# First out-projection tile written out by hand with its own w_out stages; context-convolution taps and gate products kept in written order

## The chip, the cores and the metric

The kernel runs on one core of a Trainium2 chip. A core has five engines with queues of their own: TensorE (PE, matrix products), VectorE (DVE), ScalarE (ACT), GpSimd (POOL) and SyncE (SP, which here issues most of the transfers). Each engine works through its own list of instructions in order; between engines, semaphores hold an instruction until what it needs is there. The metric is the device time of one execution in microseconds, and lower is better. The kernel before takes 1871.06 us in the median of 3 runs (1869.57 to 1874.34).

## What is computed

One layer of a hybrid network on 256 context tokens and 2048 latent tokens, all in float32. An input projection gives six groups of columns; a state-space branch (SSD, with a short convolution and two scan directions) and a conformer branch (a gated convolution of width 31 and a layer norm) are computed from them and meet in one output projection with w_out:

```python
h = rms_norm(x, g_pre) * (1 + scale) + shift
u = h @ w_in
z, xbc, dt_raw, ga, gb, gsil = jnp.split(u, [I_Z, I_XBC, I_DT, I_GA, I_GB], axis=-1)
y_ssd, h_fin = ssd_branch(z, xbc, dt_raw, ssd_conv_w, ssd_conv_b, a_log, dt_bias, d_skip, ssd_norm_g, h0)
y_conf = conformer_branch(ga.reshape(bsz, rows, cols, D_CONF), gb.reshape(bsz, rows, cols, D_CONF),
                          conf_conv_w, conf_conv_b, conf_ln_g, conf_ln_b)
y_conf = y_conf.reshape(bsz, seqlen, D_CONF) * jax.nn.silu(gsil)
out = jnp.concatenate([y_ssd, y_conf], axis=-1) @ w_out
return x + gate * rms_norm(out, g_post), h_fin
...
def conformer_branch(ga, gb, conv_w, conv_b, ln_g, ln_b):
    h = ga * jax.nn.sigmoid(gb)
    h = depthwise_conv(h, conv_w, conv_b)
    h = layer_norm(h, ln_g, ln_b)
    return jax.nn.silu(h)
```

The outputs are the context rows, the latent rows and the final states of the context's two scans.

## The kernel before

The 2304 tokens are 18 tiles of 128 (0 and 1 are context) and, for the input projection, five blocks (`TOK`, `BNS`: one of 256 tokens, four of 512) in two halves, `ORDER = ((1, 2, 0), (3, 4))`. A float32 product is three products of rounded parts (high by high, low by high, high by low; L391 to L393 in the input projection, `out_part`, L1136, in the output projection, where all instructions of the stage carry L77, the line of the helper that records them). So each operand is cast (ACT) and its rest subtracted (DVE).

For each half the columns come in units of 128: the xbc columns with their 5-tap convolution, then `gab_unit` (eight units; gb, then ga for each block, with the product gth at L555), then `silu_unit` for z and gs (L567, L568). `load_w` brings the columns: in the first half from w_in, split on the chip and kept in DRAM; in the second half by two loads wh and wl (L359, L360) from there. Beside these units generators run in alternation: the scan of the SSD branch (L663 to L795), the latent convolution on PE (cp, L648, evicted by DVE as cvv, L652, and stored at L657), `gate_rows` (products of w_mod columns wg for the gate, L576 to L581) and `ctx_conv` (L600 to L613: for each of eight channel groups, cg is loaded at L602, the first tap is L606 and thirty more are L608, all on DVE).

The scheduler of the language decides the order of each engine's list from a simulated time line, and may move one instruction ahead of another that was written first. The exception is what is recorded through `InOrder` while its flag `on` is set: that stays behind the instruction of its engine recorded before it. The flag is set for the loop over output tiles only (L1243 on).

Behind the second half, `w_out` is brought in 16 row blocks k by `load_wo` (L965 to L977): a load to wst, a cast to woh on ACT, a subtraction to wol on DVE. Blocks 0 to 8 are loaded before the three last silu units (gs columns 5 to 7, run first over block 3 for all three, then over block 4); blocks 9 to 15 at L1224, behind them, when the buffers of the input projection are closed. The tiles of the output projection run from 17 down. Each needs, for its SSD half, the state product qo and decay, the gate with z, the squares' sums over channels (zr, then pm on PE, rstd, pn on PE), and for its conformer half cn, its mean (cm), centring, squares (nq), scale, silu and the gate with gs. Tile 17 is prepared among and behind the last silu units, tile 16 behind them (L1226 to L1242); every later tile is prepared in the loop while its predecessor's 16 k-steps run on PE. The state of the backward context scan is written at the very end (`state_out(1, ...)`, L1316).

PSUM has 3 banks for the unit products ("mm") and 5 for the rest. `SLOT = (0, 1, 2, 1, 2)` says in which of three buffers a block's input lies; such a buffer is closed when the last unit that reads it has run, and its room goes to the pools of the output projection (p2 for the conformer tiles, p3 for output tiles).

## Time and profile before

| what | value |
|---|---|
| median of 3 runs | 1871.06 us (1869.57 to 1874.34) |
| the profiled execution, its own time | 1872.28 us |
| span of the profiled execution | 1870.5 us |
| mean granted TensorE clock | 0.984 |
| ACT busy, POOL busy | 863.8 us (46%), 175.9 us (9%) |
| HBM traffic over the span | 200 GB/s |
| last stage, last silu matmul to the end | 1404.90 to 1870.5 us |

The page lists each engine's busy time. PE is a list of matmuls that follow each other at a fixed pitch; where it stands still, the waits view names the tile that it wanted and the instruction or transfer that gave it. A row of the timeline is start, duration, engine, line and operation, output<-inputs, and in brackets the idle time ahead of it with what ended it. The windows view cuts the span into stretches. Its column PEclk is the clock that TensorE was granted as a share of full speed. SPq rows are DMA issues on SP's queue.

### The profile page before, as it was taken

How to read it: one execution, taken by the hardware profiler on the slowest of the kernel's cores; microseconds unless marked ns; L12 is line 12 of the kernel's file. 1: busy time of each engine (PE TensorE's matmuls, PEld its weight loads, DVE VectorE, ACT ScalarE, POOL GpSimd, SP SyncE). 2: the span in 40 equal slices, each digit the busy share in tenths (PEclk: the TensorE clock that was granted, in tenths of full speed). 3: DMA queues.
4: the chain of work that ended last, by engine and by line, in shares of the span. 5: the costliest groups of instructions: out<-in, count | busy, mean ns of one | idle time of the engine just before them, and what ended most of it. 6: DMA issues, size and time to landing. Idle time of an engine off the chain costs nothing.

```text
span 1870.5 us, 30012 instructions
## 1 busy us (share of the span) xinstructions
PE 1808.1 (97%) x11223; PEld 1493.1 (80%) x11223; DVE 1203.1 (64%) x1841; ACT 863.8 (46%) x1956; POOL 175.9 (9%) x281
## 2 busy tenths in 40 slices
...
GB/s 298 219 199 210 203 241 181 175 254 219 195 217 211 226 196 169 167 155 189 170 200 233 199 251 229 258 244 175 331 189 209 183 167 174 172 171 178 182 106 79
DMA packets 305309, 375.22 MB, mean 201 GB/s; under 512 B 85254, under 2 KB 204678, under 8 KB 305164
## 3 DMA queue, kind: packets, MB, share of 16 engines
...
q14 instruction: 57, 0.47, 0.1%
HBM read 243.66 MB, written 129.59 MB: 200 GB/s over the span
## 4 chain that ended last, share of the span: by engine, by line
PE 85%; DMA 7%; DVE 4%; ACT 1%; issue 1%; SPq 1%; POOL 0%; POOLq 0%; DVEq 0%; ACTq 0%
PE op L77 21%; PE sp L391 7%; PE sp L392 7%; PE sp L393 7%; PE xp L391 5%; PE xp L392 5%; PE xp L393 5%; PE ga L391 3%; PE ga L393 2%; PE ga L392 2%; PE gb L391 2%; PE gb L393 2%; PE gb L392 2%; DMA lb<-lt 2%; PE py L732 2%; DVE cg L608 2%
## 5 line engine op out<-in xcount | busy, mean ns | idle before, releaser
L696 ACT ACTIVATE lb<-lb,WB 128x128 f32<-128x128 f32 x576 | 184.3, 391 | 167.7 <-POOL lb L688 162.1
L391 PE MATMUL sp<-hh,wh 128*128 128x512 f32 (+1 forms) x640 | 238.5, 373 | 0.0
L392 PE MATMUL sp<-hl,wh 128*128 128x512 f32 (+1 forms) x640 | 236.0, 369 | 0.0
L393 PE MATMUL sp<-hh,wl 128*128 128x512 f32 (+1 forms) x640 | 235.8, 368 | 0.0
L391 PE MATMUL xp<-hh,wh 128*128 128x512 f32 (+1 forms) x480 | 179.3, 375 | 6.1 <-ACT wh L366 4.9
L688 POOL TENSOR_SCALAR_AFFINE_SELECT lb<-lb 128x512 f32<-128x512 f32 x144 | 112.6, 786 | 714.2 <-ACT el L685 366.7
L393 PE MATMUL xp<-hh,wl 128*128 128x512 f32 (+1 forms) x480 | 179.0, 373 | 0.0
L392 PE MATMUL xp<-hl,wh 128*128 128x512 f32 (+1 forms) x480 | 178.9, 373 | 0.0
L488 DVE SCALAR_TENSOR_TENSOR cva<-raw,cwh,cva 128x1280 f32<-128x1280 f32 (+1 forms) x96 | 142.1, 1488 | 19.7 <-ACT cva L482 17.9
L391 PEld LDWEIGHTS sp<-hh,wh 128*128 128x128 f32 x640 | 120.6, 189 | 20.8 <-DVE sth L568 0.4
L393 PEld LDWEIGHTS sp<-hh,wl 128*128 128x128 f32 x640 | 120.6, 188 | 20.7
L392 PEld LDWEIGHTS sp<-hl,wh 128*128 128x128 f32 x640 | 120.7, 189 | 19.8
L391 PE MATMUL ga<-hh,wh 128*128 128x512 f32 (+1 forms) x320 | 122.0, 381 | 6.8 <-DMA wh<-whd 6.3
L391 PE MATMUL gb<-hh,wh 128*128 128x512 f32 (+1 forms) x320 | 121.4, 379 | 5.3 <-DVE gth L555 5.3
L393 PE MATMUL ga<-hh,wl 128*128 128x512 f32 (+1 forms) x320 | 119.4, 373 | 0.5 <-DMA wl<-wld 0.5
L392 PE MATMUL gb<-hl,wh 128*128 128x512 f32 (+1 forms) x320 | 119.6, 374 | 0.0
L393 PE MATMUL gb<-hh,wl 128*128 128x512 f32 (+1 forms) x320 | 119.6, 374 | 0.0
L392 PE MATMUL ga<-hl,wh 128*128 128x512 f32 (+1 forms) x320 | 119.2, 373 | 0.0
L568 DVE SCALAR_TENSOR_TENSOR sth<-sth,sp 128x512 f32<-128x512 f32 (+1 forms) x80 | 50.4, 630 | 97.3 <-ACT sth L567 96.9
L391 PEld LDWEIGHTS xp<-hh,wh 128*128 128x128 f32 x480 | 92.1, 192 | 23.2 <-ACT wh L366 5.5
L608 DVE SCALAR_TENSOR_TENSOR cg<-cg,cv 128x256 f32<-128x256 f32 x240 | 107.6, 487 | 0.6
L392 PEld LDWEIGHTS xp<-hl,wh 128*128 128x128 f32 x480 | 91.7, 191 | 15.7 <-DVE hl L312 0.4
...
## 6 DMA issues: line engine op xcount, KB each, us to landing
lb<-lt ACTq DMA_DIRECT2D x144, 256.0 KB, 4.5
...
```

The lines of the kernel that those rows point to most:

```text
L77: return lambda *a, **k: self._tc.keep_in_program_order(f(*a, **k))
L391: T.matmul(ps[:, :BN], wh[:, k, :], hh[:, k, :], start=(k == 0), stop=False)
L392: T.matmul(ps[:, :BN], wh[:, k, :], hl[:, k, :], start=False, stop=False)
L393: T.matmul(ps[:, :BN], wl[:, k, :], hh[:, k, :], start=False, stop=(k == KT - 1))
L488: V.scalar_tensor_tensor(a[:, :n], raw[:, t:t + n], cwh[:, ct * 5 + t:ct * 5 + t + 1], a[:, :n], MUL, ADD)
L568: V.scalar_tensor_tensor(th, th, 1.0, ps[:, :BN], ADD, MUL)
L608: V.scalar_tensor_tensor(acc, g[:, t:t + 256], cv[:, w0 + t:w0 + t + 1], acc, MUL, ADD)
L688: G.affine_select(E[g, hq, d], E[g, hq, d], pattern=[[0, 4], [sg, P]], compare_op=ALU.is_ge, fill=NEG, base=0, channel_multiplier=-sg)
L696: S.activation(lb[:, h, :], lb[:, h, :], AF.Exp, bias=WB[:, i, c + h:c + h + 1])
L732: T.matmul(py[g][j * HD:(j + 1) * HD, q * P:(q + 1) * P], xt[g][:, h * HD:(h + 1) * HD], E[g, hq, 0][:, t, :], start=True, stop=True)
```

## The change

1. `InOrder` gets `here`, which keeps one instruction in written order without the flag. The gate products and the taps of `ctx_conv` use it.
2. `SLOT` becomes (0, 1, 2, 2, 1): blocks 3 and 4 exchange their buffers. The last two z units of the first half run over blocks 2, 1, 0 in place of 1, 2, 0, and the last silu units of the second half over block 4 first and then block 3, so that block 4, with tiles 14 to 17, is finished one pass earlier, and p2 is opened between the two passes.
3. `load_wo` is cut into `wo_load` and `wo_split`, and w_out 9 to 15 get staging buffers of p3.
4. Tile 16's SSD part and both conformer tiles' loads, sums, means and squares are written among the last silu units, tile 15's SSD loads too.
5. The first output tile is written out ahead of the loop, with the splits of w_out 9 to 15 between its k-steps. In the second and third tile (`e` 4 and 2) the stages come 4 and 2 k-steps later than in the rest.
6. `state_out(1, ...)` is written inside the tile before the last.

```diff
-SLOT = (0, 1, 2, 1, 2)
+SLOT = (0, 1, 2, 2, 1)
...
+    def here(self, name, *a, **k):
+        return self._tc.keep_in_program_order(getattr(self._eng, name)(*a, **k))
...
-                    V.scalar_tensor_tensor(acc[a][:, :D], wg, sc[:, a, k:k + 1], acc[a][:, :D], MUL, ADD)
+                    V.here("scalar_tensor_tensor", acc[a][:, :D], wg, sc[:, a, k:k + 1], acc[a][:, :D], MUL, ADD)
...
-            V.scalar_tensor_tensor(acc, g[:, t:t + 256], cv[:, w0 + t:w0 + t + 1], acc, MUL, ADD)
+            V.here("scalar_tensor_tensor", acc, g[:, t:t + 256], cv[:, w0 + t:w0 + t + 1], acc, MUL, ADD)
...
+            tag = ("gg", "xr", "o", "o")[k % 4]
+            wst[k] = p3.tile([P, D], F32, tag=tag, name=f"wst{k}", bufs=2 if tag == "o" else 1)
...
+    i1 = order[1]
+    ssd_load(i1)
+    st_load(i1)
...
-    last = [silu_unit(1, GS0, GS, j, hb) for j in range(5, 8)]
+    last = [silu_unit(1, GS0, GS, j, hb, (4, 3)) for j in range(5, 8)]
     for b in range(2):
         for m, u in enumerate(last):
             run(take(u, 8))
             if b == 0 and m == 1:
                 rs = norms(i, yz, None)
-            if b == 1 and m == 0:
+                state_mm(i1)
+                y_state(i1)
+                y_gate(i1)
+            if b == 0 and m == 2:
                 ssd_scale(i, yz[0], spread(i, rs))
                 yh = hl(p0, "y", 2, i, yz[0])
                 lo(yh)
+                yz = y_sum(i1)
...
                 ph_b[1].close()
                 p2 = ph_1.enter_context(tc.tile_pool(name="p2", bufs=1))
-                n = conf_load(i)
-                v, t = conf_sum(i, n)
-                conf_centre(n, conf_mean(i, t))
+                nn = [conf_load(i), conf_load(i1)]
+                vv = [conf_sum(j, n) for j, n in zip((i, i1), nn)]
...
+                nq = conf_sqsum(i, vv[0][0])
+            if b == 1 and m == 0:
+                rs = norms(i, None, nq)
+                nq = conf_sqsum(i1, vv[1][0])
...
-    for k in range(9, 16):
-        load_wo(k, wo4)
+    for k in range(9, 13):
+        wo_load(k, wo4)
...
+    banks(i)
+    out_part(pso[i], yh, 0, 1)
+    rs = norms(nxt, yz, nq)
+    out_part(pso[i], yh, 1, 4)
...
+    out_part(pso[i], yh, 5, 8)
+    for k in (9, 10):
+        wo_split(k)
+        wo_load(k + 4, wo4)
+    v = nq[0]
+    conf_silu(n, v)
+    out_part(pso[i], pt, 8, 9)
+    v2, t = conf_sum(nx2, n2)
+    wo_split(11)
+    wo_load(15, wo4)
+    for k in range(12, 15):
+        wo_split(k)
+    load_gg(0)
+    out_part(pso[i], pt, 9, 12)
+    mean = conf_mean(nx2, t)
+    y_state(nx2)
+    state_decay(nx2, 0)
+    wo_split(15)
...
+    for a, i in enumerate(order[1:], 1):
         last = a + 1 == NT
+        e = {1: 4, 2: 2}.get(a, 0)
...
+        out_seg(i, yh, pt, 8 + e, 10 + e)
+        if a + 2 == NT:
+            state_out(1, Sb, lambda n: p1.tile([P, D], F32, tag="z", name=n, bufs=2)[:, 0:512])
...
-    state_out(1, Sb, lambda n: p1.tile([P, D], F32, tag="z", name=n, bufs=2)[:, 0:512])
```

Each engine has the same number of instructions as before. Three places of the lists follow; a row is line, operation, output<-inputs and shape, and lines from L75 on stand some lines further down in the changed kernel (L77 there is L81, L555 is L559; `here` is L75).

PE's list before, from the end of the last silu unit on (pm and pn are the sums and the spread of the norms of tile 17 or 16, qo16 tile 16's state product, cm16 its mean, op17 the first output tile, zr16 and nq16 the sums of tile 16's squares):

```order
L1059 MATMUL pm17_13676<-ones_218,nq17_13672 128x1
L1070 MATMUL pn17_13682<-ident_209,yr171_13680 128x128
L1014 MATMUL qo160_13762<-ct16_13749,Sb0_13062 128x128 x4
L1014 MATMUL qo161_13763<-ct16_13749,Sb1_13063 128x128 x4
L1107 MATMUL cm16_13801<-v16_13797,ones_218 128x128
L77 MATMUL op17_0_13822<-woh0_13065,yh17_13584 128x512
L77 MATMUL op17_1_13823<-woh0_13065,yh17_13584 128x512
L77 MATMUL op17_0_13822<-wol0_13064,yh17_13584 128x512
L77 MATMUL op17_1_13823<-wol0_13064,yh17_13584 128x512
L77 MATMUL op17_0_13822<-woh0_13065,yl17_13585 128x512
L77 MATMUL op17_1_13823<-woh0_13065,yl17_13585 128x512
L77 MATMUL pm16_13833<-ones_218,zr16_13777 128x1
```

PE's list in the changed kernel: first the piece between two of the silu units over block 4, where tile 16's state product now stands; then the end of the last silu unit.

```order
L397 MATMUL sp1_4640_6_4_13507<-hh4_7330,wl5408_1_13416 128x512
L1072 MATMUL pm17_13532<-ones_218,zr17_13284 128x1
L1027 MATMUL qo160_13538<-ct16_13306,Sb0_13062 128x128 x4
L1027 MATMUL qo161_13539<-ct16_13306,Sb1_13063 128x128 x4
L395 MATMUL sp1_4640_7_4_13553<-hh4_7330,wh5536_1_13479 128x512
```

```order
L397 MATMUL sp1_4640_7_3_13725<-hh3_7120,wl5536_1_13478 128x512
L81 MATMUL op17_0_13791<-woh0_13065,yh17_13581 128x512
L1072 MATMUL pm17_13662<-ones_218,nq17_13629 128x1
L1083 MATMUL pn17_13701<-ident_209,yr171_13666 128x128
L81 MATMUL op17_1_13792<-woh0_13065,yh17_13581 128x512
L81 MATMUL op17_0_13791<-wol0_13064,yh17_13581 128x512
L81 MATMUL op17_1_13792<-wol0_13064,yh17_13581 128x512
L81 MATMUL op17_0_13791<-woh0_13065,yl17_13582 128x512
L81 MATMUL op17_1_13792<-woh0_13065,yl17_13582 128x512
L81 MATMUL pm16_13799<-ones_218,zr16_13585 128x1
L81 MATMUL pm16_13799<-ones_218,nq16_13668 128x1
L81 MATMUL op17_0_13791<-woh1_13091,yh17_13581 128x512
```

The norm of tile 17's conformer half now stands within the first k-step, and the state product and mean of tile 16 no longer stand ahead of it; the sums pm16 still stand behind the first k-step.

DVE's list before, in the first half, around the first tap (L606) of the third channel group, cg2, and the product gth of the gab unit 3, block 2:

```order
L773 TENSOR_TENSOR yg11_2948<-yg11_2948,py11_3150 128x512
L606 TENSOR_SCALAR cg2_4773<-cg2_4773,cv_214,cfb2_250 128x256
L775 TENSOR_TENSOR yg11_2948<-yg11_2948,yo11_3225 128x512
L608 SCALAR_TENSOR_TENSOR cg2_4773<-cg2_4773,cv_214 128x256 x2
L795 TENSOR_TENSOR btl2_3299<-pb2_3228,bth2_3298 128x256
L608 SCALAR_TENSOR_TENSOR cg2_4773<-cg2_4773,cv_214 128x256
L721 TENSOR_TENSOR xw200_3424<-xt20_3304,WS_259 128x512
L555 SCALAR_TENSOR_TENSOR gth0_3_2_3195<-gth0_3_2_3195,ga0_3_2_3197 128x512
L608 SCALAR_TENSOR_TENSOR cg2_4773<-cg2_4773,cv_214 128x256
```

The same place in the changed kernel:

```order
L777 TENSOR_TENSOR yg11_2948<-yg11_2948,py11_3150 128x512
L779 TENSOR_TENSOR yg11_2948<-yg11_2948,yo11_3225 128x512
L799 TENSOR_TENSOR btl2_3299<-pb2_3228,bth2_3298 128x256
L725 TENSOR_TENSOR xw200_3424<-xt20_3304,WS_259 128x512
L559 SCALAR_TENSOR_TENSOR gth0_3_2_3195<-gth0_3_2_3195,ga0_3_2_3197 128x512
L705 TENSOR_TENSOR lb2000_3170<-lb2000_3170,cb2_3300 128x512
L705 TENSOR_TENSOR lb2010_3246<-lb2010_3246,cb2_3300 128x512
L705 TENSOR_TENSOR lb2100_3327<-lb2100_3327,cb2_3300 128x512
L727 TENSOR_TENSOR xwl200_3426<-xw200_3424,xwh200_3425 128x512
L772 TENSOR_TENSOR yg21_3519<-xT2_3102,dcol_246 128x512
```

The first tap of the third group and its followers are no longer here; in the changed list they stand behind the last taps of group two.

DVE's list before, early in the second half's gab units, between two product rows gth; cvv0 is the eviction of the latent convolution's product cp0:

```order
L608 SCALAR_TENSOR_TENSOR cg4_8920<-cg4_8920,cv_214 128x256
L608 SCALAR_TENSOR_TENSOR cg5_10011<-cg5_10011,cv_214 128x256
L652 SCALAR_TENSOR_TENSOR cvv0_8673<-cp0_0_8674,cbb_8324 128x8x64
L652 SCALAR_TENSOR_TENSOR cvv0_8673<-cp0_1_8675,cbb_8324 128x8x64
L608 SCALAR_TENSOR_TENSOR cg4_8920<-cg4_8920,cv_214 128x256
L608 SCALAR_TENSOR_TENSOR cg5_10011<-cg5_10011,cv_214 128x256
```

And in the changed kernel, from the same state product's operand xwl901 on:

```order
L727 TENSOR_TENSOR xwl901_8640<-xw901_8638,xwh901_8639 128x512
L725 TENSOR_TENSOR xw910_8768<-xt91_8584,WS_259 128x512
L559 SCALAR_TENSOR_TENSOR gth1_1_3_8510<-gth1_1_3_8510,ga1_1_3_8512 128x512
L656 SCALAR_TENSOR_TENSOR cvv0_8673<-cp0_0_8674,cbb_8324 128x8x64
L656 SCALAR_TENSOR_TENSOR cvv0_8673<-cp0_1_8675,cbb_8324 128x8x64
L755 TENSOR_TENSOR Sf0_260<-Sf0_260,eTf_253 128x512
L757 TENSOR_TENSOR yo90_8882<-po90_8759,el90_8426 128x512
L759 TENSOR_TENSOR Sf0_260<-Sf0_260,pst900_8764 128x512
L727 TENSOR_TENSOR xwl910_8770<-xw910_8768,xwh910_8769 128x512
L725 TENSOR_TENSOR xw911_8885<-xt91_8584,WS_259 128x512
L704 TENSOR_TENSOR lb10000_8950<-lb10000_8950,lb10001_8952 128x512
L656 SCALAR_TENSOR_TENSOR cvv0_8673<-cp0_2_8790,cbb_8324 128x8x64
```

There are sixteen alternating taps of the groups cg4 and cg5 in front of cvv0 before, of which the fence shows the last two; in the changed kernel cvv0 stands straight behind gth1_1_3.

More of the change, by code (lines that the diff above doesn't have):

```diff
@@ L919, in backbone_kernel @@
     interleave(post(0, 6), merge(scan(range(9)), 68, extra, 9 + 4 * 13), 90 * 8)
-    last = [silu_unit(0, GS0, GS, j, hb, (1, 2, 0)) for j in (6, 7)]
+    last = [silu_unit(0, GS0, GS, j, hb, (2, 1, 0)) for j in (6, 7)]
     prep = hprep(3, hb)
@@ L963, in backbone_kernel, with wo_load, wo_split @@
     WH, WL = {}, {}
-    def load_wo(k, pool):
-        wl = pool.tile([P, D], F32R, name=f"wol{k}", tag=f"wol{k}")
-        wh = pool.tile([P, D], F32R, name=f"woh{k}", tag=f"woh{k}")
-        wr = p0.tile([P, D], F32, tag=("yh", "yl")[k % 2], name=f"wst{k}", bufs=2)
-        DMA.dma_start(wr, w_out[k * P:(k + 1) * P, :])
+    wst = {}
+    def wo_load(k, pool):
+        WL[k] = pool.tile([P, D], F32R, name=f"wol{k}", tag=f"wol{k}")
+        WH[k] = pool.tile([P, D], F32R, name=f"woh{k}", tag=f"woh{k}")
+        if k < 9:
+            wst[k] = p0.tile([P, D], F32, tag=("yh", "yl")[k % 2], name=f"wst{k}", bufs=2)
+        else:
+            tag = ("gg", "xr", "o", "o")[k % 4]
+            wst[k] = p3.tile([P, D], F32, tag=tag, name=f"wst{k}", bufs=2 if tag == "o" else 1)
+        DMA.dma_start(wst[k], w_out[k * P:(k + 1) * P, :])
+    def wo_split(k):
+        wl, wh, wr = WL[k], WH[k], wst.pop(k)
         if k < 8:
@@ L1207, in backbone_kernel @@
                 lo(yh)
+                yz = y_sum(i1)
+                for g in range(2):
+                    state_decay(i1, g)
                 ph_b[1].close()
                 p2 = ph_1.enter_context(tc.tile_pool(name="p2", bufs=1))
-                n = conf_load(i)
-                v, t = conf_sum(i, n)
-                conf_centre(n, conf_mean(i, t))
+                nn = [conf_load(i), conf_load(i1)]
+                vv = [conf_sum(j, n) for j, n in zip((i, i1), nn)]
+                for (v, t), j, n in zip(vv, (i, i1), nn):
+                    conf_centre(n, conf_mean(j, t))
+                    conf_square(v, n)
+                nq = conf_sqsum(i, vv[0][0])
+            if b == 1 and m == 0:
+                rs = norms(i, None, nq)
+                nq = conf_sqsum(i1, vv[1][0])
+            if b == 1 and m == 1:
+                n, v = nn[0], vv[0][0]
+                conf_scale(n, spread(i, rs))
+                conf_silu(n, v)
+                ssd_load(order[2])
+            if b == 1 and m == 2:
+                gs0, v0, n = gs_load(i), v, nn[1]
     for u in last:
         run(u)
-    v, nq = conf_sqsum(i, conf_square(v, n))
-    conf_scale(n, spread(i, norms(i, None, (v, nq))))
-    gs = gs_load(i)
-    conf_silu(n, v)
-    conf_gate(v, gs)
     ph_b[2].close()
```

83 lines of the change are left out of this document (46 added, 37 removed).

## The prediction

> **What bounds the kernel now.** First the engines' shares on the page and its chain, then PE's waits, then the span cut into stretches at those waits.
>
> ```profile
> span 1870.5 us, 30012 instructions
> PE 1808.1 (97%) x11223; PEld 1493.1 (80%) x11223; DVE 1203.1 (64%) x1841; ACT 863.8 (46%) x1956; POOL 175.9 (9%) x281
> PE 85%; DMA 7%; DVE 4%; ACT 1%; issue 1%; SPq 1%; POOL 0%; POOLq 0%; DVEq 0%; ACTq 0%
> PE pm L77 <- DVE zr L986: 12.3, 1, 12.3
> PE ga L391 <- DMA wh<-whd: 6.3, 2, 5.5
> PE gb L391 <- DVE gth L555: 5.3, 2, 3.8
> PE px L708 <- issue: 4.1, 2, 2.7
> PE cp L648 <- DVE yg L773: 3.8, 1, 3.8
> PE cp L648 <- DVE cvv L652: 1.5, 2, 1.1
> ```
>
> TensorE is the bound: it stands still for 1870.5 - 1808.1 = 62.4 us, and the change adds and removes no matmul. So all that can be won is idle time of PE and time in which PE ran at half clock. The columns of the next view are the stretch, its length, the busy time of PE, PEld, DVE, ACT and POOL, the granted clock, the DMA share and GB/s.
>
> ```profile
> 360.00:380.00 20.00, 16.20 (x90) 14.15 (x89) 13.73 (x26) 9.05 (x23) 2.90 (x7) 0.83 0.61 199
> 380.00:950.00 570.00, 567.49 (x3014) 475.20 (x3013) 330.28 (x496) 261.56 (x572) 48.46 (x79) 1.00 0.59 197
> 950.00:1110.00 160.00, 141.68 (x1420) 110.42 (x1419) 122.92 (x235) 68.40 (x170) 20.30 (x29) 0.95 0.89 214
> 1110.00:1404.90 294.90, 294.70 (x2697) 237.40 (x2695) 159.18 (x238) 132.02 (x305) 27.09 (x36) 1.00 0.80 239
> 1404.90:1447.56 42.66, 29.52 (x146) 24.84 (x144) 33.89 (x44) 28.32 (x61) 2.67 (x3) 0.84 0.78 211
> 1447.56:1860.00 412.44, 412.44 (x2003) 346.73 (x2002) 291.50 (x439) 192.09 (x488) 43.39 (x49) 1.00 0.57 159
> ...
> 367.95:374.78 6.83, 5.55 (x14) 4.34 (x15) 6.83 (x14) 3.61 (x10) 0.00 (x0) 0.50 0.62 207
> 965.29:968.70 3.41, 3.41 (x32) 2.21 (x16) 3.41 (x9) 0.32 (x1) 0.00 (x0) 0.50 0.31 72
> 1030.14:1036.97 6.83, 5.82 (x117) 4.96 (x118) 6.83 (x15) 6.13 (x19) 2.09 (x2) 0.50 0.47 154
> 1091.58:1098.41 6.83, 6.17 (x14) 4.52 (x15) 1.98 (x3) 2.45 (x8) 0.50 (x1) 0.50 1.02 376
> 1412.43:1426.09 13.66, 3.89 (x11) 3.33 (x12) 7.21 (x14) 9.61 (x17) 0.00 (x0) 0.50 1.05 268
> ```
>
> Three places are left to win at. Idle time is length less PE busy: 3.8 us in 360 to 380, 18.3 us in 950 to 1110, 13.1 us in 1404.90 to 1447.56, 2.5 us in 380 to 950, and as good as none elsewhere behind 64 us. The last five rows are the stretches at clock 0.50; half of PE's busy time in each is lost: 2.8, 1.7, 2.9, 3.1 and 1.9 us.
>
> **The first out-projection tile** (the largest term). The PE rows of the transition from the last silu unit to tile 17:
>
> ```profile
> 1404.90 0.28 PE L1059 MATMUL pm<-ones,nq 128*128 128x1 f32 x2
> 1406.06 0.49 PE L1070 MATMUL pn<-ident,yr 128*128 128x128 f32 x2 [0.88 <-POOL yr L148]
> 1406.38 1.95 PE L1014 MATMUL qo<-ct,Sb 128*128 128x128 f32 x16
> 1422.20 0.56 PE L77 MATMUL pm<-ones,zr 128*128 128x1 f32 x2 [12.26 <-DVE zr L986]
> 1447.10 0.62 PE L77 MATMUL op<-woh,pl 128*128 128x512 f32 x2
> 1447.56 0.61 PE L77 MATMUL op<-woh,yh 128*128 128x512 f32 x2
> 1416.28 1.23 DVE L1134 SCALAR_TENSOR_TENSOR v<-v,gsl 128x1024 f32<-128x1024 f32 x1 [3.70 <-DMA gsl<-gs]
> 1417.42 2.36 DVE L976 TENSOR_TENSOR wol<-wst,woh 128x1024 fp32r<-128x1024 f32 x2
> 1421.77 0.28 DVE L986 TENSOR_TENSOR zr<-z 128x128 f32<-128x128 f32 x1
> 1418.67 1.48 SPq L969 DMA_DIRECT2D wst<-in_w_out  x2
> 1423.73 1.04 ACT L975 CAST woh<-wst 128x1024 fp32r<-128x1024 f32 x1 [3.77 <-DMA wst<-in_w_out]
> ```
>
> PE does the first k-step of tile 17 from 1408.3 and then waits 12.26 us for tile 16's norms, because tile 16's scale, gate and sums, and two halves of w_out, stand on DVE in front of the last sum (zr, 1421.77), which itself stood 3.70 us behind a load of gsl. The changed order has qo16 inside the silu units, with tile 16's gate and sum, and cm17 and cm16 29 and 27 matmuls before the last silu one, 6.6 us at the 0.227 us pitch below. So when PE reaches pm16, in front of k-step 1, its inputs are long there, and the 12.26 us go, and with them the half clock, 1.9 us. What is moved does not vanish: qo16 and cm16, 1408.31 - 1406.38 = 1.93 us by the starts (1406.38 above, and k-step 0 is 3 pairs long), are still paid, only earlier.
>
> What is late next? The pitch of one pair of matmuls is 1447.56 - 1447.10 = 0.46, in the mean 0.453, so the tile's 48 pairs are 21.8 us; pm17, the 0.88 us wait for the norm and pn17, pm16, pn16, qo15 and cm15 make about 4.2 us more, and k-step 9 is due some 16.3 us behind the last silu matmul, k-step 15 some 25 us. The loads of w_out 9 to 12 are still issued only when the last silu matmul has released its buffers. Two such loads issued from 1418.67 were there at 1423.73, 5.1 us later; four, 2.1 MB at the 268 GB/s of 1412 to 1426, take about 8 us. Then one cast on ACT (1.04) and one subtraction on DVE (2.36 / 2 = 1.18) each. I put DVE's row from there in its written order at 1.15 to 1.2 us for each full-width row: tile 16's scale to 8.9, gate of tile 17 to 10.1, conformer scale, the two low halves to 13.6, w_out 9 to 14.8, 10 to 15.9, then a sum, 11 to 14 to 22.0, y_state, 15 to 25.6. So 9 is 1.5 us early and 15 some 0.6 us late. Term: -12.26 - 1.9 + 0.6 = **-13.6 us**. Ends: -16 (the 0.88 goes too, and more of the norms is hidden), and -6 if the w_out row is 7.5 us late.
>
> **The context convolution's taps, first half.** Before, the scheduler interleaves the taps of two convolutions and puts a group's first tap ahead of other work.
>
> ```profile
> 364.94 0.41 DVE L606 TENSOR_SCALAR cg<-cg,cv,cfb 128x256 f32<-128x256 f32 x1 [6.15 <-DMA cg<-gl]
> 956.37 6.41 DVE L608 SCALAR_TENSOR_TENSOR cg<-cg,cv 128x256 f32<-128x256 f32 x16
> 1024.06 0.68 DVE L753 TENSOR_TENSOR yo<-po,el 128x512 f32<-128x512 f32 x1
> 1024.84 0.63 PE L708 MATMUL px<-ident,xT 128*128 128x128 f32 x4 [2.67 <-issue]
> ```
>
> At 364.94 DVE has stood 6.15 us for the load of cg, and gth (L555), six rows behind, is what gb waits 3.8 us for, with 2.8 us of half clock behind it. In the new order the taps of one group stand behind those of the group ahead of it, and the third group's load is issued more than a hundred DVE rows before its first tap. That wait goes. Its bounds: all 6.6 us and the 2.5 us of 380 to 950 (-9), or another load takes the place (gate products, now pinned, wait for wg; +1). I take 6.6 + 1.0 less 1.1 for a small wait in its place: **-6.5 us**.
>
> **950 to 1110**, 18.3 us idle and 1.7 + 2.9 + 3.1 = 7.7 us of half clock. The 16 taps at 956.37 stand ahead of cvv, for which cp waits (1.5 us, then 1.7 of half clock); in the new order cvv stands straight behind gth and no tap is ahead: -3.1. The px waits (4.1 us, the releaser not named) look like waits for a PSUM bank: the longer ends at 1024.84, 0.1 us behind DVE's L753, which reads po and stands among taps; the taps of the fifth group begin later now but still run here: half, -2. The 3.8 + 2.9 us at yg are a DVE wait for the load of yp, with taps only between: I take -1.5. The 5.47 us of ga (and 3.1 of half clock) are SP's:
>
> ```profile
> 1075.61 5.01 SPq L657 DMA_DIRECT2D cv<-cvv  x4
> 1084.18 0.38 SPq L359 DMA_DIRECT2D wh<-whd  x1
> ```
>
> The load of wh stands behind four stores of cvv, and it still does in the new order: 0. Term: **-6.6 us**; ends -18 (all but the ga wait and a little) and +3 (cp and yg wait as before and the moved DMAs make one more such wait).
>
> The Trainium skill, "TensorE: Matmul & The Clock Gate", section "What's actually happening", says that the clock falls to half after at least one idle window of about 3.4 us, a window that runs freely. The 3.80 us wait agrees; the 3.41 us at clock 0.50 from 965.29 do not, since PE had stopped there for only 1.15 and 0.30 us. By that rule the 1.7 us there come from something other than the wait and stay, and the forecast would be 1.7 us higher.
>
> **The end.**
>
> ```profile
> 1862.84 1.03 PE L162 MATMUL so<-ident,Sb 128*128 128x128 f32 x8
> 1863.04 0.60 ACT L77 ACTIVATE o<-op 128x512 f32<-128x512 f32 x1 [3.35 <-PE op L77]
> ```
>
> The eight state transposes ran beside the last tile's squares, so they cost nothing; moved into tile 16 they stand in PE's row before the end: **+1.0 us**. The shift of the norms by 4 and 2 k-steps in tiles 16 and 15 I cost at 0: 1447 to 1860 has no idle PE, and DVE, 291.50 of 412.44 busy, has room; without that cover one late norm costs about the 0.88 us above. Gate products, tap order and slot exchange remove no instruction; on DVE (64% busy) they are hidden as long as nothing urgent stands behind them. For new waits that a rewritten order always can have I add **+3 us**, about one wait of the size of the gb or yg one (0 to 10).
>
> **Sum.** -13.6 - 6.5 - 6.6 + 1.0 + 3 = -22.7 us, from 1872.28 of the profiled execution 1849.6. That execution lies 1.2 us above the median of the runs, 1871.06, so the median forecast is 1871.06 - 22.7 = **1848.4 us**.
>
> **The rivals.**
> - *Only the transition pays* (0.16): the taps that go from one place come up at another, because DVE is 123 of 160 us busy in 950 to 1110 and does the same work. 1871.1 - 13.6 + 1.0 = 1858.5.
> - *The wait becomes one for w_out* (0.09): loads 9 to 15 begin behind the last silu matmul, and three of them wait for a buffer that a subtraction frees. Late by 7.5 us, beyond the 0.6 assumed: about 1855.9 with the rest as forecast.
> - *Everything but the ga wait goes* (0.08): -18 and -9 in place of -6.6 and -6.5, and no new wait: 1871.1 - 13.6 - 9 - 18 + 1 = 1831.5.
> - *Slower* (0.05): gate products and taps are now pinned, so DVE stands at them when their load is late, with gth and cvv queued behind. One such stand cost 3.8 + 2.8 = 6.6 us at 364.94. There are 8 loads of wg and 8 of cg; with the three gains at -26.7 + 1.0, four of them (26.4) bring it level and six (39.6) give about 1885. Against it: the changed order issues the cg loads long before their first taps, the first group's apart, and wg has three buffers.
> - *The change doesn't do what it says* (0.05): the wait for tile 16's norms moves to pn16 or to the second tile and gives most of the 13.6 back, the rest balanced; about 1869, within 0.3%.
>
> The forecast's own case, 1840 to 1856, has the remaining 0.57. The range 1834 to 1862 holds it and the first two rivals, 0.82. Faster by more than 0.3% (5.6 us, about what a measurement of this kernel tells from no change): 0.57 + 0.16 + 0.09 + 0.08 = 0.90; within: 0.05; slower: 0.05.
>
> **What would show it.** Right: no PE wait over 1.5 us between the last silu matmul and the second out tile, that window about 27 us long and at clock 1.00; no wait of DVE at the first tap for cg<-gl, and no gb wait; ga near 1092 still waiting about 5 us. Wrong: PE waits on wol 9 to 15 in tile 17; DVE rows of the gate products or first taps with "<-DMA wg" or "<-DMA cg" and a PE wait on gth or cvv right behind; an idle sum in 950 to 1110 near 18 us as before.

## The result and the profile after

The changed kernel takes 1860.74 us in the median of 7 runs (1854.66 to 1866.34), against 1872.56 us for the kernel before in the 7 runs that were compared with it: a ratio of 0.9935, 95% interval 0.9919 to 0.9952, so 11.8 us less (1872.56 - 1860.74). The forecast was 22.7 us less. The measured time lies within the range given, and only about half of the sum came. Times are medians of all runs of a kernel, ratios leave out two executions at a lower granted clock: 2965.21 us (0.558) with the state at the end, and 1968.6 us (0.861) with the stores on ACT's queue.

The page of the changed kernel's profile (this execution took 1866.34 us, the longest of the seven), with the span, PE and DVE, and a selection of PE's waits behind them (what PE waited for, then us in total, times, and the longest):

```profile
span 1864.3 us, 29991 instructions
PE 1809.9 (97%) x11223; PEld 1492.7 (80%) x11223; DVE 1211.3 (65%) x1841; ACT 865.3 (46%) x1956; POOL 168.4 (9%) x281
PE px L712 <- issue: 6.4, 3, 2.9
PE ga L395 <- DMA wh<-whd: 6.1, 1, 6.1
PE po L743 <- DVE yg L777: 3.2, 1, 3.2
PE cp L652 <- DVE yg L777: 2.8, 1, 2.8
PE gb L395 <- DVE gth L559: 2.4, 2, 2.1
PE pst L749 <- ACT sb L765: 1.3, 1, 1.3
PE op L81 <- DVE wol L81: 1.1, 1, 1.1
PE pn L1083 <- POOL yr L152: 0.9, 1, 0.9
```

The wait of 12.3 us at pm is gone, and so is the larger of the two gb waits. The ga wait is still there, and px waits are longer than before (6.4 in place of 4.1 us). The waits at po and pst have grown: before they were 0.96 and 0.81 us, now they are 3.2 us (po, for yg) and up to 1.3 us (pst). The windows view, cut at the starts of the stages (the first gb matmul of a half, the first silu matmul, the end of the last one, the second output tile), shows where:

```profile
232.51:504.24 271.73, 269.37 (x1502) 223.99 (x1501) 176.85 (x276) 115.12 (x283) 25.15 (x45) 0.99 0.59 195
...
907.84:1178.66 270.82, 252.48 (x2452) 199.80 (x2451) 159.13 (x266) 116.24 (x278) 28.41 (x47) 0.96 0.86 217
1178.66:1411.74 233.08, 227.55 (x1849) 183.49 (x1848) 149.12 (x239) 99.40 (x226) 17.15 (x22) 0.99 0.75 232
1411.74:1440.40 28.66, 26.12 (x126) 21.05 (x126) 22.43 (x28) 19.13 (x35) 2.14 (x3) 1.00 0.82 276
1440.40:1856.75 416.35, 416.35 (x2023) 349.71 (x2021) 296.14 (x446) 196.46 (x497) 43.47 (x49) 1.00 0.56 159
...
1120.11:1123.52 3.41, 3.41 (x10) 2.63 (x9) 1.31 (x2) 1.82 (x5) 0.64 (x1) 0.50 1.04 393
1195.20:1198.62 3.42, 3.18 (x10) 2.73 (x11) 1.34 (x3) 0.76 (x3) 0.64 (x1) 0.50 0.40 133
1277.12:1280.54 3.42, 3.29 (x10) 2.84 (x11) 3.35 (x7) 2.18 (x6) 0.64 (x1) 0.50 0.17 63
```

The same cut for the kernel before, for the changed one, and for those runs that the argument rests on. Each entry is the stage's length, and in brackets PE's idle time in it and half of PE's busy time at clock 0.50, all from the traces (us). A column is one execution: that of the changed kernel is the longest of its seven, its second profile (1860.64 us) lies near the median, and that of "groups 4 to 7 free" (1848.73 us) is the shortest of its four.

| stage | before | changed | changed, second profile | no holds | holds alone | groups 4 to 7 free | most taps of 4 to 7 left out |
|---|---|---|---|---|---|---|---|
| gab units, first half | 277.2 (6.3, 2.8) | 271.7 (2.4, 1.7) | 270.8 (2.6, 0) | 278.7 (7.8, 2.8) | 269.5 (1.3, 0) | 267.8 (0, 0) | 271.2 (3.0, 0) |
| gab units, second half | 269.7 (18.3, 7.7) | 270.8 (18.3, 8.4) | 267.9 (17.6, 5.9) | 265.8 (17.8, 4.6) | 265.2 (14.6, 6.8) | 266.1 (14.7, 7.9) | 269.6 (18.1, 8.3) |
| silu units, second half | 221.8 (0.2, 0) | 233.1 (5.5, 3.2) | 230.9 (4.7, 1.4) | 224.9 (0.9, 0) | 228.7 (6.0, 0) | 223.5 (0, 0) | 225.0 (1.2, 0) |
| tile 17 | 42.5 (13.1, 1.9) | 28.7 (2.5, 0) | 29.2 (3.0, 0) | 28.0 (2.1, 0) | 43.1 (13.0, 2.7) | 28.7 (2.5, 0) | 28.0 (2.1, 0) |
| other tiles | 415.4 | 416.3 | 416.4 | 416.3 | 415.4 | 416.3 | 416.3 |

The first two columns give the account: first half -5.5, gab units of the second half +1.2, its silu units +11.3, tile 17 -13.8, other tiles +0.9. The silu units hold 1.9 us that only moved there (qo16 and cm16), and 8.6 us of waits and half clock that are new. These sum to -5.9 us. The second profile of the same kernel has -6.5, -1.8, +9.1, -13.3 and +0.9, in sum -11.6, about what the medians differ by.

### The profile page after: what moved, and what is told of

Read it like the earlier page. It is cut to its first block, busy times and chain, and to the rows that moved or that the text cites. A ratio compares the mean times of both kernels' runs of the same rounds, so it can differ in the third digit from the quotient of the medians.

```text
span 1864.3 us, 29991 instructions
## 1 busy us (share of the span) xinstructions
PE 1809.9 (97%) x11223; PEld 1492.7 (80%) x11223; DVE 1211.3 (65%) x1841; ACT 865.3 (46%) x1956; POOL 168.4 (9%) x281
## 4 chain that ended last, share of the span: by engine, by line
PE 75%; DMA 12%; DVE 4%; issue 4%; ACT 3%; POOL 1%; SPq 1%; ACTq 0%; POOLq 0%; DVEq 0%
PE op L81 20%; PE sp L395 6%; DMA lb<-lt 6%; PE sp L396 6%; PE sp L397 6%; PE xp L395 4%; PE xp L396 4%; PE xp L397 4%; PE gb L395 2%; PE gb L397 2%; PE gb L396 2%; PE ga L395 2%; PE ga L396 2%; PE ga L397 2%; PE py L736 1%
## 5 line engine op out<-in xcount | busy, mean ns | idle before, releaser
L692 POOL TENSOR_SCALAR_AFFINE_SELECT lb<-lb 128x512 f32<-128x512 f32 x144 | 105.7, 737 | 736.2 <-ACT el L689 412.0
L75 DVE SCALAR_TENSOR_TENSOR cg<-cg,cv 128x256 f32<-128x256 f32 x240 | 121.2, 505 | 3.4
L704 DVE TENSOR_TENSOR lb<-lb,lb 128x512 f32<-128x512 f32 x72 | 51.2, 711 | 92.9 <-ACT lb L700 77.1
```

Source lines behind the costliest of these rows:

```text
L75: return self._tc.keep_in_program_order(getattr(self._eng, name)(*a, **k))
L692: G.affine_select(E[g, hq, d], E[g, hq, d], pattern=[[0, 4], [sg, P]], compare_op=ALU.is_ge, fill=NEG, base=0, channel_multiplier=-sg)
L704: V.tensor_tensor(a, a, E[g, hq, 1], ADD)
```

## The experiments

**The parts apart.** Four kernels: the changed one with `here` made an ordinary call; the one before with `here` on gate products and taps; the changed one with the taps of the second half free; and the changed one again.

```diff
     def here(self, name, *a, **k):
-        return self._tc.keep_in_program_order(getattr(self._eng, name)(*a, **k))
+        return getattr(self._eng, name)(*a, **k)
```

> The changed kernel with gate products and taps free again; all of the out-projection part stays. Theory A (the out-projection part gives about 12 us; the held taps win some 6 us in the first half and give as much back behind 1110 us, where they now stand ahead of yo and so hold a PSUM bank that px wants): the gb wait of 3.8 us near 369 and the cvv wait near 963 are back, no px wait over 1 us between 1110 and 1410, ratio to before about 0.993 to 0.995, like the changed kernel. Theory B (the new waits behind 1110 come from the order of the DMA issues, not from the taps): px waits of 1.7 to 2.9 us stay there, and the ratio is about 0.998.

Measured 1860.05 us, ratio 0.9935 (0.9909 to 0.9961), as with the holds. PE's waits in its profile:

```profile
PE gb L395 <- DVE gth L559: 6.4, 2, 5.6
PE px L712 <- issue: 5.3, 2, 3.3
```

The gb wait of the first half is back, the px waits of over 1 us behind 1110 us are gone (the two in the second line lie at 983 and 1025). The cvv wait near 963 did not come back, so that it is gone does not hang on the holds alone. What the holds together are worth in the changed kernel is too little to be seen in the ratio.

```diff
-                    V.scalar_tensor_tensor(acc[a][:, :D], wg, sc[:, a, k:k + 1], acc[a][:, :D], MUL, ADD)
+                    V.here("scalar_tensor_tensor", acc[a][:, :D], wg, sc[:, a, k:k + 1], acc[a][:, :D], MUL, ADD)
...
-            V.scalar_tensor_tensor(acc, g[:, t:t + 256], cv[:, w0 + t:w0 + t + 1], acc, MUL, ADD)
+            V.here("scalar_tensor_tensor", acc, g[:, t:t + 256], cv[:, w0 + t:w0 + t + 1], acc, MUL, ADD)
```

> The kernel before with gate products and taps held in written order and nothing else. Theory A: no gb wait near 369, first half about 6 us shorter, px waits behind 1110 of together about 6 us with half clock behind them; 12.3 us at pm as before; ratio about 0.998 to 1.002. Theory B: the 6 us stay won, ratio about 0.996.

Measured 1868.73 us, ratio 0.9982 (0.9968 to 0.9997). The first half's gab units are 7.8 us shorter than before and the second half's silu units 6.8 us longer; the wait at pm is untouched, 12.2 us. So both halves of theory A are there without any change to the output projection. Two things it did not have: the silu units lose by waiting alone (6.0 us, no half clock), and the gab units of the second half are 4.5 us shorter, so that not all of the gain is given back.

```diff
-        V.here("tensor_scalar", acc, g[:, 0:256], cv[:, w0:w0 + 1], cfb2[:, j:j + 1], MUL, ADD)
+        pin = V.here if j < 4 else lambda name, *x: getattr(V, name)(*x)
+        pin("tensor_scalar", acc, g[:, 0:256], cv[:, w0:w0 + 1], cfb2[:, j:j + 1], MUL, ADD)
...
-            V.here("scalar_tensor_tensor", acc, g[:, t:t + 256], cv[:, w0 + t:w0 + t + 1], acc, MUL, ADD)
+            pin("scalar_tensor_tensor", acc, g[:, t:t + 256], cv[:, w0 + t:w0 + t + 1], acc, MUL, ADD)
```

> The changed kernel with the taps of the second half (groups 4 to 7) free again; gate products and the taps of groups 0 to 3 stay held. Theory A: the first half keeps its 6 us, the px waits behind 1110 go (9 us idle and 5 us of half clock in the profiled execution), some of the old waits of 960 to 1090 come back (up to 10 us); ratio to before about 0.989 to 0.993. Theory B: as the changed kernel, 0.9935.

Measured 1854.29 us, ratio 0.9901 (0.9872 to 0.9929). The first half keeps its gain, the silu units of the second half stand still no more: the windows of its profile from 907 us to the last silu matmul.

```profile
907.00:1110.00 203.00, 189.39 (x1657) 150.00 (x1656) 147.28 (x267) 83.56 (x204) 22.84 (x37) 0.95 0.87 224
1110.00:1394.50 284.50, 283.45 (x2637) 228.74 (x2635) 158.94 (x238) 129.41 (x301) 24.63 (x32) 1.00 0.79 237
```

Behind 1110 us PE is idle for 1.1 us, where the changed kernel's profile has 8.9 (291.00 us, 282.09 busy, from 1110 to 1401).

> The changed kernel again, for a second profile. If the waits behind 1110 hang on the order of the lists (A), px waits stand at the same three places (near 1110, 1195 and 1277) and sum to over 4 us; if they hang on how the transfers happen to fall (B), they stand elsewhere or are gone when the execution is one of the short ones (1855). Ratio 0.992 to 0.995.

Measured 1859.95 us, ratio 0.9933 (0.9914 to 0.9952). The lines of its waits view to which the larger waits behind 1110 us belong (each line counts the whole span):

```profile
PE px L712 <- DVE cvv L656: 3.3, 2, 2.7
PE pst L749 <- ACT sb L765: 2.6, 2, 2.4
PE px L712 <- issue: 1.7, 1, 1.7
```

Not all at the same places: of the three px waits, the one near 1190 (1.7 us) is there again, one of 2.7 us has come at 1235, those near 1110 and 1277 are not. The sum from 1110 to the last silu matmul is alike (8.3 us of single waits over 0.6 us, against 9.9). So with this order such waits come in both profiles, at places that differ from run to run; the expectation that they sit at fixed places was wrong.

What makes such a wait is seen in the changed kernel at 1277, DVE's rows and the px row of PE:

```profile
1274.95 1.00 DVE L75 SCALAR_TENSOR_TENSOR cg<-cg,cv 128x256 f32<-128x256 f32 x2
1275.86 0.68 DVE L755 TENSOR_TENSOR Sf<-Sf,eTf 128x512 f32<-128x512 f32 x1
1276.46 0.68 DVE L757 TENSOR_TENSOR yo<-po,el 128x512 f32<-128x512 f32 x1
1277.25 1.09 PE L712 MATMUL px<-ident,xT 128*128 128x128 f32 x4 [2.88 <-issue]
```

yo is the row that reads po, a product in one of the five banks from which px takes its own. It ends at 1276.46 + 0.68 = 1277.14, and px starts 0.1 us later; in front of it stand taps of the last group. The view names no releaser, but in all 29 px waits over 0.3 us of this kind in the fourteen profiles a yo row ends 0.1 us before px starts. In the changed kernel the three waits lie where the taps of groups 5, 6 and 7 stand (1065 to 1111, 1168 to 1208, 1260 to 1295 us). Taps are not always needed for a px wait: the one at 1235 of the second profile lies between groups 6 and 7 (1204.7 and 1254.8 us) and ends with cvv.

**The taps' load or the taps' place?** The changed kernel with 27 of the 30 later taps of each of groups 4 to 7 left out.

```diff
-            V.here("scalar_tensor_tensor", acc, g[:, t:t + 256], cv[:, w0 + t:w0 + t + 1], acc, MUL, ADD)
+            if j < 4 or t < 4:
+                V.here("scalar_tensor_tensor", acc, g[:, t:t + 256], cv[:, w0 + t:w0 + t + 1], acc, MUL, ADD)
```

> The changed kernel with 27 of the 30 further taps of each of the groups 4 to 7 left out (the context's second four channel groups get a convolution of 4 taps), all else as in the changed kernel. Theory A (wherever those taps stand on DVE, yo and the evictions stand behind some of them, and PE waits for their banks): no PE wait over 1 us between 1110 us and the last silu matmul, and the px waits of 960 to 1030 gone too; the second half 10 to 15 us shorter than in the changed kernel; ratio about 0.985 to 0.988. Theory B (the waits come from transfers): the waits stay, ratio 0.991 to 0.9935.

Measured 1855.76 us, ratio 0.9904 (0.9889 to 0.9919). Its windows:

```profile
950.00:1110.00 160.00, 144.75 (x1345) 113.04 (x1333) 79.46 (x127) 72.58 (x182) 18.56 (x31) 0.95 0.86 218
1110.00:1200.00 90.00, 86.33 (x923) 68.47 (x924) 51.57 (x83) 46.41 (x118) 12.72 (x18) 0.98 0.86 240
1200.00:1402.00 202.00, 201.69 (x1729) 163.78 (x1728) 114.33 (x170) 86.78 (x191) 11.97 (x16) 1.00 0.78 238
```

A split answer. Behind 1200 us the waits are gone, as theory A has it, and the kernel is as fast as the one with the same taps free, no faster: leaving most of them out wins no more than moving them. But from 950 to 1200 PE still stands still for 18.9 us (15.25 + 3.67), though DVE is busy for only 79.46 of 160 us. One of these waits is again at px, 3.32 us at 1111.36. There the waits don't hang on the taps, and theory A as stated for them falls.

**Which hold wins the first half?** The changed kernel with only the gate products held, and the one with groups 4 to 7 free with the gate products free as well.

```diff
-            V.here("scalar_tensor_tensor", acc, g[:, t:t + 256], cv[:, w0 + t:w0 + t + 1], acc, MUL, ADD)
+            V.scalar_tensor_tensor(acc, g[:, t:t + 256], cv[:, w0 + t:w0 + t + 1], acc, MUL, ADD)
```

> The changed kernel with all taps free, only the gate products held. If the taps' hold alone won the first half: gb wait of 3 to 6 us near 369 as without any hold, first half like before, ratio as without holds, 0.9935. If the gate products' hold won it: no gb wait, about 0.990.

```diff
-                    V.here("scalar_tensor_tensor", acc[a][:, :D], wg, sc[:, a, k:k + 1], acc[a][:, :D], MUL, ADD)
+                    V.scalar_tensor_tensor(acc[a][:, :D], wg, sc[:, a, k:k + 1], acc[a][:, :D], MUL, ADD)
```

> Groups 4 to 7 free and the gate products free as well; only the taps of groups 0 to 3 held. If the taps' hold won the first half: as with the gate products held, 0.990, no gb wait over 1.5 us near 369. If the gate products' hold won it: gb wait of 3 to 6 us, ratio 0.9935.

Gate products alone: 1864.73 us, ratio 0.9943 (0.9927 to 0.9960). The gb wait near 369 did not come back and the time was no better for it, which neither case had; a px wait of 5.27 us at 413, again behind a yo row, and more stand in its place, and the gab units of the first half take 282.6 us (in an execution of 1873.03 us, the longest of the five). Taps of groups 0 to 3 alone: 1855.17 us, ratio 0.9899 (0.9884 to 0.9914), 269.7 us there, gb wait 1.2 us. In the ten profiles with these taps held and three PSUM banks for the unit products that stage takes 267.8 to 271.7 us, in the three without the hold 277.2 to 282.6 us. The first half is won by holding the taps; the gate products' hold adds nothing that can be measured.

**The state's place.**

```diff
-        if a + 2 == NT:
-            state_out(1, Sb, lambda n: p1.tile([P, D], F32, tag="z", name=n, bufs=2)[:, 0:512])
...
     V.on = S.on = T.on = False
+    state_out(1, Sb, lambda n: p1.tile([P, D], F32, tag="z", name=n, bufs=2)[:, 0:512])
```

> Groups 4 to 7 free, and the state written at the very end again as before. The eight transposes run beside the last tile's squares, so the tile stage is 0.9 us shorter and the tail is no longer: ratio 0.0005 below that of the kernel with groups 4 to 7 free (0.9901). Rival: the state's two stores then are the last transfers, and the tail grows by what is won.

Measured 1854.09 us, ratio 0.9890 (0.9873 to 0.9906). The ratio can't tell 0.9 us, the trace does: the stage of the other tiles is 415.4 us in place of 416.3, and the tail behind the last out-projection matmul 7.5 us in both.

**What bounds the gab units of the second half?** Three kernels, each against one of the causes that the waits there name: SP's queue, the transfers themselves, the PSUM banks. All three have groups 4 to 7 free as well, and the third also the state at the end and the split of w_out 15 written earlier, as in the faster version below.

```diff
-            DMA.dma_start(CV[c0:c0 + 32, 256:].rearrange("c (r w) -> r c w", w=64), vt[u * 32:(u + 1) * 32])
+            nc.scalar.dma_start(CV[c0:c0 + 32, 256:].rearrange("c (r w) -> r c w", w=64), vt[u * 32:(u + 1) * 32])
```

> Groups 4 to 7 free, and the stores of cvv issued on ACT's queue instead of SP's. If ga's wait for wh near 1080 (5.3 us in the kernel with groups 4 to 7 free, with half clock behind it) comes from SP's queue, where wh's load stands behind four such stores, it shrinks to under 1.5 us and the ratio falls to 0.986 or 0.987. If it comes from the transfers' own length (load on the DMA engines, share 0.9 there), it stays at 4 to 6 us and the ratio at 0.990.

Measured 1862.09 us, ratio 0.9944 (0.9925 to 0.9963): slower than without the edit (0.9901, though the intervals still touch). Two PE rows of it:

```profile
1080.83 0.50 PE L397 MATMUL ga<-hh,wl 128*128 128x512 f32 x1 [0.69 <-DMA wl<-wld]
1119.10 0.68 PE L653 MATMUL cp<-cx,kt 32*32 32x64 f32 x32 [4.17 <-ACT sb L766]
```

ga's wait fell to 0.69 us. The load of wh is now issued 4.6 us behind the first load of kd in front of it (1067.67 to 1072.22), where the kernel with groups 4 to 7 free has 9.5 us (1062.41 to 1071.91), so SP's queue did hold it. But that load of kd, which waits for ACT's kt, itself comes 5.3 us later here, and PE reaches ga 5 us later: the load of wh goes out no earlier than before. Behind it cp waits 4.17 us for an eviction on ACT, and idle time in the stage rose to 22.1 us.

```diff
             DMA.dma_start(flat(wh), WHD[t])
+            if GA0 <= c0 < GB0 + 1024 and c0 < GS0 and c0 >= GA0:
+                return wh, wh
             DMA.dma_start(flat(wl), WLD[t])
```

> Groups 4 to 7 free, and the loads of wl for the sixteen gb and ga columns of the second half left out (wh stands in for wl in the product, so gb and ga are computed with a wrong low part of the weights). 8 MB less are moved between 910 and 1180 us. If the transfers are what bounds the second half's gab units (14.7 us idle and 7.9 us of half clock in the kernel with groups 4 to 7 free), idle and half clock there fall below 12 us together and the ratio to 0.985 or less; if it is the scan's own chain through DVE, ACT and PSUM banks, they stay above 18 us and the ratio at 0.989 to 0.990.

This kernel leaves out the low part of those weights. Measured 1859.27 us, ratio 0.9936 (0.9919 to 0.9954); 950 to 1110 in its profile:

```profile
950.00:1110.00 160.00, 142.14 (x1309) 111.64 (x1308) 117.21 (x217) 68.99 (x174) 20.79 (x30) 0.95 0.75 180
```

The DMA share fell from 0.87 to 0.75 and the rate from 223 to 180 GB/s (the kernel with groups 4 to 7 free, same window), and PE is still idle for 17.9 us there. The ratio did not fall either; if anything it rose from 0.9901. The amount moved is not the bound.

```diff
-        return psp.tile([P, 512], F32, tag=tag, name=name, bufs=3 if tag == "mm" else 5)
+        return psp.tile([P, 512], F32, tag=tag, name=name, bufs=2 if tag == "mm" else 6)
...
-        pso[i] = [bank("ss" if i % 2 and q else "mm", f"op{i}_{q}") for q in range(2)]
+        pso[i] = [bank("ss" if i % 2 else "mm", f"op{i}_{q}") for q in range(2)]
```

> The kernel with groups 4 to 7 free, the state at the end and the earlier split of w_out 15, with the PSUM banks shared out as 2 for the unit products and 6 for the rest (before 3 and 5; odd output tiles then take both their banks from the rest). If the second half's gab units wait because the scan's steps want banks (px and cp waits that end with yo, yg or an eviction), idle and half clock there fall from 25 us to under 15 and the ratio to 0.985 or less. If the chain of the scan itself bounds them, they stay at 20 to 28 us and the ratio at 0.989 to 0.991. Two banks for the unit products could make PE wait for evictions in the silu units, which would show as sp waits there and nowhere else.

Measured 1895.7 us, ratio 1.0115 (1.0088 to 1.0142). The waits at px are gone, and others are there:

```profile
PE ga L395 <- DVE gth L559: 13.0, 6, 4.3
PE sp L395 <- DVE sth L572: 8.8, 5, 3.3
PE py L737 <- DVE lb L706: 7.9, 2, 4.6
```

Two banks are too few for the unit products, which costs more than the sixth bank gives; idle time and half clock in the gab units of the second half are 31.2 us (21.2 + 10.0), not less. As an answer on banks it is not clean, since both shares changed at once.

**A faster version.** Groups 4 to 7 free, the state at the end, and in the first tile:

```diff
     mean = conf_mean(nx2, t)
+    wo_split(15)
     y_state(nx2)
     state_decay(nx2, 0)
-    wo_split(15)
```

> Groups 4 to 7 free, the state written at the very end, and in the first output tile the split of w_out 15 written ahead of y_state and the state's decay. In the changed kernel PE waits 0.55 us for woh 15 and 1.11 us for wol 15 there, behind 2.02 us of decay on ACT and 2.4 us of y_state on DVE. If these are what is late, both waits go, the tile takes 1.4 us less, and the ratio is 0.9885 (0.989 with the state at the end alone). If the load of w_out 15 is what is late, they stay.

Measured 1851.29 us, ratio 0.9899 (0.9881 to 0.9916). Tile 17 takes 27.5 us in place of 28.4; the waits for woh 15 and wol 15 are 0.22 and 0.53 us in place of 0.55 and 1.11, smaller but not gone, and one of 0.7 us at pm of the second tile has come. The stage of the other tiles takes 416.35 us in place of 415.45 with the state at the end alone, so what tile 17 gains is lost there; the ratio expected, 0.9885, was not reached. This kernel and the other three with groups 4 to 7 free and the transfers as they were (0.9890 to 0.9901) are faster than both kernels of the case by their medians, and can't be told from each other; for the first of them (0.9901) the interval still overlaps that of the changed kernel.

## Why the prediction was right, and where its sum was not

The sum was -22.7 us and -11.8 came, so the measured time lies outside the forecast's own case (1840 to 1856); it lies within the range only because that was drawn to hold the first two rivals. By the second profile, with the 1.9 us of qo16 and cm16 counted to the first tile, the terms are: first tile -11.4 (forecast -13.6), first half -6.5 (-6.5), gab and silu units of the second half together +5.4 (-6.6 + 3 = -3.6), the end +0.9 (+1.0).

**First tile, forecast -13.6.** Right in its mechanism, some 2 us too large. The stage became 13.8 us shorter (13.3 in the second profile), but the 1.9 us of qo16 and cm16 only left it for the silu units: -11.9 and -11.4. PE's rows of tile 17 in the changed kernel, and those of ACT and DVE that make its last waits:

```profile
1412.96 0.49 PE L1083 MATMUL pn<-ident,yr 128*128 128x128 f32 x2 [0.88 <-POOL yr L152]
1414.44 0.28 PE L81 MATMUL pm<-ones,zr 128*128 128x1 f32 x2
1437.52 0.73 PE L81 MATMUL op<-woh,ph 128*128 128x512 f32 x2 [0.55 <-ACT woh L81]
1439.37 0.73 PE L81 MATMUL op<-wol,ph 128*128 128x512 f32 x2 [1.11 <-DVE wol L81]
1440.40 0.62 PE L81 MATMUL op<-woh,yh 128*128 128x512 f32 x2
1434.37 2.02 ACT L81 ACTIVATE Sb<-Sb,eTb 128x64 f32<-128x64 f32 x8
1436.42 1.05 ACT L81 CAST woh<-wst 128x1024 fp32r<-128x1024 f32 x1
1433.41 1.05 ACT L81 CAST woh<-wst 128x1024 fp32r<-128x1024 f32 x1 [1.41 <-DMA wst<-in_w_out]
1434.49 1.23 DVE L81 TENSOR_TENSOR wol<-wst,woh 128x1024 fp32r<-128x1024 f32 x1 [1.23 <-ACT woh L81]
1438.09 1.22 DVE L81 TENSOR_TENSOR wol<-wst,woh 128x1024 fp32r<-128x1024 f32 x1
```

pm for tile 16 waits for nothing, the 0.88 us are the same to the hundredth, and the clock is 1.00 throughout (the window of the stage). What waits last is w_out 15, as the row worked out by hand had it; it is 1.66 us late and not 0.6, because I had put no time in that row for the loads of 13 and 14. The row is right as far as 9, done 14.8 us behind the last silu matmul; then the cast of 14 waits 1.41 us for its load and DVE 1.23 us for the cast, so 14 is done after 24.0 us in place of 22.0, and 15 after 27.6 in place of 25.6. The decay on ACT, ahead of the cast of 15, makes the 0.55 us at woh. Of the 1.7 to 2.2 us by which the term was too large these waits are 1.1 (1.5 in the second profile); the rest is not traced to a row. Moving that split ahead took 1.0 us off the stage, and the stage behind it became 0.9 us longer. The rival of a w_out wait of 7.5 us did not come.

**First half, forecast -6.5.** Measured -5.5 and -6.5. The wait is the one given. Without the holds DVE stands at a first tap for cg and gb waits as long, 5.62 us; in the changed kernel (last row) no first tap stands in front of gth, and it waits for no load:

```profile
367.93 0.41 DVE L75 TENSOR_SCALAR cg<-cg,cv,cfb 128x256 f32<-128x256 f32 x1 [5.62 <-DMA cg<-gl]
372.09 0.80 PE L395 MATMUL gb<-hh,wh 128*128 128x512 f32 x1 [5.62 <-DVE gth L559]
364.90 0.68 DVE L559 SCALAR_TENSOR_TENSOR gth<-gth,ga 128x512 f32<-128x512 f32 x1
```

With the holds alone the wait goes too. It is not the only way in which free taps cost there, as the kernel with only the gate products held shows (px at 413).

**950 to 1110, forecast -6.6, and new waits, +3.** This is the step that failed. Taken together, the gab and silu units of the second half were to become 3.6 us shorter; less the 1.9 us moved there they became 10.5 us longer in one profile and 5.4 in the other. In the window 950 to 1110 itself idle time fell by 3.4 us (160.00 - 145.04 = 15.0 in place of 18.3), but as much came up behind 1110, in the same units. Two parts of the step were wrong:
- "no tap is ahead: -3.1" and the half of the px waits: the waits named did go, but the stage did not get shorter. 18.3 us idle were 18.3 and 17.6 afterwards, and still 18.1 with most of the taps left out. Others took their place, at po, pst and px (1.7 us at 1110.55), and the one at cp for yg stayed with 2.8 of 3.8 us. The taps stood in front of what PE waited for, and did not bound the stage.
- "+3 us, about one wait": the held taps spread over the stage behind, where before there was no tap and no wait. DVE's taps alone by window, before and then changed:

```profile
950.00:1000.00 50.00, 23.26 (x54) 0.97 0.91 189
1250.00:1300.00 50.00, 0.00 (x0) 1.00 0.63 196
```

```profile
950.00:1000.00 50.00, 12.92 (x27) 1.00 0.89 243
1250.00:1300.00 50.00, 15.49 (x31) 0.97 0.59 182
```

  There yo and evictions stand among them, and the silu units pay 8.6 us (5.9 in the second profile, 4.1 of it the wait at 1235 with its half clock, where no tap stands). With those taps free PE stands idle there for 0 to 1.2 us in the four kernels with transfers and banks as they were, and for 1.5 and 2.0 us in the two with other transfers. That the hold costs these units some us is shown, but not that a tap stands behind each wait.

So the first rival's price, 1858.5, was nearest to what was measured, and its reason ("the taps that go from one place come up at another") held for the second half alone, with the first half's gain and a loss of about the same size side by side.

**The ga wait, forecast 0.** Right (6.1 us, 5.5 in the second profile), and SP's queue has a part in it: without the stores in front the load follows the kd loads 4.9 us sooner and the wait is 0.69 us. But PE came 5 us later in that kernel, and the stage gains nothing.

**The end, +1.0.** Measured +0.9, and back by moving the state.

**The clock gate's rule.** The Trainium skill, "TensorE: Matmul & The Clock Gate", section "What's actually happening", asks for an idle window of about 3.4 us before the clock is halved. The changed kernel's rows at 0.50 from 1120.11, 1195.20 and 1277.12 each stand at waits of 0.86, 1.81 and 2.88 us. So the trace differs here again. The 3.80 us wait, which the prediction took to agree, does so by its length only: it began at 365.43 (369.23 - 3.80) and the clock fell at 367.95, 2.5 us into it. Not each such wait has half clock behind it: in the changed kernel 1.68 us at 1110.55 and 1.34 us at 1148.07 left the clock at 1.00. What decides is not shown; where the clock does fall, a short wait costs more than its length.

**What stays open.** What holds the gab units of the second half at 21 to 27 us of idle time and half clock in every kernel run here but the two that raised it to 31 and 33. It is not the number of taps, not the amount that the transfers move, and not the stores in SP's queue alone, since each was taken away and the sum did not fall. The scan's own chain over PE, ACT, DVE and POOL would explain that removing one wait brings up the next, but no run here shows it. Nor does any run take the out-projection part to pieces: without the holds it still shortens tile 17 by 14.5 us (42.5 to 28.0), but how much of that needs the exchanged buffers, the staging buffers of p3 or the later stages of the second and third tile is not shown.
